# Two-layer decoder trunk: both parts of the activations in one 512-column product outside the first layer, the first tile's sums in other PSUM banks, small weights of layer 2 loaded in pieces

## The chip, the cores and the metric

One Trainium2 chip; the kernel runs on one of its cores, in one launch. The metric is the device time in microseconds (us) of the whole kernel. The engines are named as the profile names them: PE (TensorE, with PEld for its weight loads), DVE (VectorE), ACT (ScalarE), POOL (GpSimd) and SP, whose queue issues nearly all DMAs.

## What is computed

256 tokens, model width 2048, everything in float32. The first layer mixes an RWKV-7 scan (16 heads of 64) and sliding-window attention; the second is a gated unit with a 128 x 128 causal product for each of 16 channel groups. Cut to what matters here:

```
h = rmsnorm(x, e_norm)                       # layer 1
z = h @ e_w_in                               # 2048 -> 6784 columns
y = concat(rwkv7(z) * silu(..), attention(z) * silu(..))
x = x + y @ e_w_out                          # 2048 -> 2048

h = rmsnorm(x, o_norm)                       # layer 2
u, v, gate = split(h @ o_w_in, 3)            # 2048 -> 3 x 2048
v = layernorm(v, sgu_ln_w, sgu_ln_b)
mixed[g] = tril(ws[g]) @ v[:, g] + bs[g]     # 16 groups of 128 channels
x = x + (u * mixed * silu(gate)) @ o_w_out
return rmsnorm(x, final_norm)
```

## The kernel before

**Products in two parts.** Each float32 operand is split into a rounded high part and the rest: a weight chunk `raw` of 128 x 1024 (512 KB, one DMA on SP's queue) becomes `wh` (ACT, a copy) and `wl` (DVE, `raw - wh`), an activation tile of 128 x 256 becomes a high and a low tile (`xh`/`xl`, `xnh`/`xnl` after the scaling of layer 1, `x1h`/`x1l` in layer 2, `yk` and `yo` for the inputs of the two output projections). A product is then the sum of three PE matmuls: `wh` by high, `wh` by low, `wl` by high. `raw`, `wh` and `wl` have three buffers each.

**Two kinds of tiles.** A "B" tile gives 128 output columns: the weights stand in the array and the 256 tokens stream through it (function `half_b`), in two chunks of 8 steps over the contracted 2048, so 48 matmuls of 256 columns for a tile. An "A" tile gives 512 output columns for both halves of the tokens (`eighth_a`): the activations stand in the array and 512 weight columns stream, 12 matmuls of 512 columns a chunk, 8 chunks, into two accumulators `psa` and `psb`. Accumulators come from the pool `acc` (3 PSUM banks of 512 float32 columns); everything else that PE writes comes from `mis` (5 banks).

**Order.** `products` walks a list of tiles: for layer 1 an A tile (keys and values), a B tile for the two small projections, 24 B tiles for the scan, 8 B, 2 A and 8 B; then `w_out` in two passes of 16 half tiles; then layer 2's `o_in`, 4 A tiles (v) and 32 B tiles (u and gate of each group in turn); then `o_out`, 16 B tiles. After each tile a function (`e_done`, `first_done`, `resid_done`, `o_done`, `last_done`) takes the sums out of PSUM. Between the chunks `pace` lets other work (`Later`) run: generators in queues, which stop at a `Hold`. A framework then orders each engine's instructions; engines are in order.

**The start.** The first A tile's sums wait in `psa` and `psb` until the row norm `rs1`/`rc1` is known; then `kv_done` copies them out on ACT (`kd`, `v`). The next tile holds the third bank. `rms_rows` computes the norm with a scratch tile `msum` in the buffer "y", which POOL's table of angles (`rope_tables`, tiles `rt`) also uses. The small products of `lora_task` (`pw`, `pa` from `hi` and `lo`) follow the norm.

**Layer 2's small weights**: `wst` (masked by POOL), `bsb`, and four rows tiles each of `lnw` and `lnb`, are loaded after `w_out` on SP's queue, between the chunks of `o_in`. `lnw`, `lnb` are needed when the 4 A tiles are done, `wst` and `bsb` by the first gate after that.

Nearly all instructions go through a counting helper, so the profile shows line 126 for them; groups are told apart by the names of their tiles.

Of the kernel before, what the change touches and what calls it, by code (L numbers as in the profile page):

```python
# [193 lines left out]
def kernel(ctx, tc, xT, w_in, w_out, o_in, o_out, cols, rows, loras, sinks, pos, ws_t, ws_b, out, dbg=None):  # L194
# [33 lines left out]
    def k1(s, tag, dt=F32):  # L228
        return t1.tile([P, 260], dt, tag=tag, bufs=2 if tag in ("kp", "rp", "vp") else 1, name=nm(s))
# [45 lines left out]
    def half_b(pss, drams, ah, al, half, first, last):  # L275
        for ps, d in zip(pss, drams):
            wh, wl = chunk(d)
            for k in range(8):
                kt = half * 8 + k
                c = slice(k * P, (k + 1) * P)  # L280
                for i, (w, a) in enumerate(((wh, ah), (wh, al), (wl, ah))):
                    TE.matmul(ps[:, 0:T], w[:, c], a(kt), start=(first and k == 0 and i == 0),
                              stop=(last and k == 7 and i == 2))

    def first_chunk(dram):
# [8 lines left out]
        for i in range(2):  # L294
            c = slice(512 * i, 512 * i + 512)
            xh_of(i)
# [4 lines left out]
    def eighth_a(ps, dram, ah, al, q):  # L301
        wh, wl = first_chunk(dram) if not seen else chunk(dram)
        for k in range(2):
            kt = 2 * q + k
            c = slice(k * 512, (k + 1) * 512)
            for h in range(2):
                t = slice(h * P, (h + 1) * P)
                for i, (w, a) in enumerate(((wh, ah), (wh, al), (wl, ah))):
                    TE.matmul(ps[h], a(kt)[:, t], w[:, c], start=(kt == 0 and i == 0),
                              stop=(kt == NK - 1 and i == 2))  # L310

    def products(order, dram, ah, al, done, lead=0, halves=(0, 1)):
# [7 lines left out]
        def tiles(ids):  # L320
            pss = [acc("ps") for _ in ids]
            for n, half in enumerate(halves):
                end = n == len(halves) - 1
                half_b(pss, [dram[base[i] + half] for i in ids], ah, al, half, n == 0, end)
# [38 lines left out]
    xh, xl = pairs_of(NK, "xh", F32R), pairs_of(NK, "xl", F32R)  # L363
# [5 lines left out]
    def xh_of(k):  # L369
        if state.get("normed"):  # L370
            return xn[k][0]
        if k not in seen:
# [3 lines left out]
            split(xh[k], xl[k], xs[:, k], col(C_GE, k))  # L376
        return xh[k]

    def xl_of(k):
        return xn[k][1] if state.get("normed") else xl[k]  # L380
# [4 lines left out]
    def scale_task():  # L385

        for q in range(8):
# [86 lines left out]
    def setup_task():  # L474
# [13 lines left out]
        blk = const.tile([P, P], F32, name="blk")  # L488
# [4 lines left out]
        G.tensor_copy(blkr, blk)  # L493
        cen = const.tile([P, P], F32, name="cen")
# [91 lines left out]
    def ch4(ap):  # L586
        return ap.rearrange("p (c l) -> p c l", c=NCH)

# [720 lines left out]
```

## Time and profile before

| what | value |
|---|---|
| median of 3 runs | 901.04 us (898.83 to 901.15) |
| the profiled execution's own time | 904.99 us |
| its span, first to last instruction | 903.2 us |
| PE busy, with PE instructions | 870.4 us (96%), 7086 |
| DVE busy | 637.8 us (71%) |
| ACT busy | 496.8 us (55%) |
| POOL busy | 123.6 us (14%) |
| mean granted PE clock | 0.98 of full speed |

Busy time of PE counts each matmul from its start to its modelled end, and neighbours overlap, so the rate is read from how many start in a stretch. The profiled execution takes 1.8 us more than its span and 4 us more than the median of the runs.

### The profile page before, as it was taken

Reading aid. Unit: us, or ns where it says so; the run is one execution under the profiler, and the core shown is the slowest. Engines: PE = TensorE matmul, PEld = TensorE weight load, DVE = VectorE, ACT = ScalarE, POOL = GpSimd, SP = SyncE. Lnnn points to the kernel's source line nnn. Section 1 sums busy time; section 2 is a strip of 40 time slices with the busy share of each in tenths; the row PEclk is TensorE's granted clock in tenths of the full one; section 3 lists DMA queues with packets and bytes.
Section 4 is the critical chain, followed back from the end, with each engine's and each line's share of the span. In section 5 each row is a group of like instructions: output and inputs, shape, how many; then the busy total and the mean of one; then the engine's idle time right before and its main releaser. Section 6 shows DMA issues by size and latency. Waiting matters only on the chain.

```text
span 903.2 us, 17601 instructions
## 1 busy us (share of the span) xinstructions
PE 870.4 (96%) x7086; PEld 818.4 (91%) x7086; DVE 637.8 (71%) x1009; ACT 496.8 (55%) x825; POOL 123.6 (14%) x212
## 2 busy tenths in 40 slices
PE   8799999999999799999999999999999999999994
PEld 7698999999998578989999978889999999999994
DVE  6699688877999856697658955559666666655553
ACT  7587666667654387987435444447434343444441
POOL 8702000000001001000007910000000000004330
PEclk9989999999999699999999999999999999999998
DMA  7535455554366221344665866655555555656642
GB/s 274 160 117 166 151 165 164 163 159 145 117 186 184 82 91 69 94 141 164 224 195 181 303 218 196 200 188 184 171 182 175 177 173 179 180 172 186 187 164 93
DMA packets 44145, 151.68 MB, mean 168 GB/s; under 512 B 5152, under 2 KB 5536, under 8 KB 43808
## 3 DMA queue, kind: packets, MB, share of 16 engines
q1 hardware_dynamic: 43344, 149.52, 51.7%
q8 instruction: 55, 0.90, 0.4%
q10 hardware_dynamic: 720, 1.05, 0.3%
q14 instruction: 26, 0.21, 0.1%
HBM read 148.45 MB, written 2.10 MB: 167 GB/s over the span
## 4 chain that ended last, share of the span: by engine, by line
PE 77%; DVE 11%; ACT 4%; POOL 4%; issue 2%; DMA 1%; SPq 0%; DVEq 0%; ACTq 0%; POOLq 0%
PE ps L126 60%; PE psa L126 5%; PE psb L126 5%; DVE wl L126 3%; DVE dd L126 1%; ACT sc L126 1%; DMA raw<-in_o_in 1%; DVE et L126 1%; PE m L126 1%; DVE tmp L126 1%; ACT wh L126 1%; PE pm L126 1%; ACT L126 1%; DVE la L126 1%; POOL rt L552 1%
## 5 line engine op out<-in xcount | busy, mean ns | idle before, releaser
L126 ACT CAST wh<-raw 128x1024 fp32r<-128x1024 f32 (+1 forms) x267 | 278.9, 1045 | 313.7 <-PE ps L126 171.7
L126 DVE TENSOR_TENSOR wl<-raw,wh 128x1024 fp32r<-128x1024 f32 (+1 forms) x267 | 329.8, 1236 | 172.1 <-ACT wh L126 170.7
L126 PE MATMUL ps<-xnh,wh 128*128 128x256 f32 x560 | 161.8, 289 | 0.0
L126 PE MATMUL ps<-xnl,wh 128*128 128x256 f32 x560 | 159.3, 285 | 1.7 <-DVE xnl L126 1.7
L126 PE MATMUL ps<-xnh,wl 128*128 128x256 f32 x560 | 159.5, 285 | 0.7 <-DVE wl L126 0.7
L126 PE MATMUL ps<-x1h,wh 128*128 128x256 f32 x512 | 146.1, 285 | 0.0
L126 PE MATMUL ps<-x1h,wl 128*128 128x256 f32 x512 | 144.9, 283 | 0.0
L126 PE MATMUL ps<-x1l,wh 128*128 128x256 f32 x512 | 144.8, 283 | 0.0
L126 PEld LDWEIGHTS ps<-xnl,wh 128*128 128x128 f32 x560 | 107.3, 192 | 2.4 <-DVE xnl L126 2.1
L126 PEld LDWEIGHTS ps<-xnh,wh 128*128 128x128 f32 x560 | 107.4, 192 | 1.9 <-issue 1.0
L126 PEld LDWEIGHTS ps<-xnh,wl 128*128 128x128 f32 x560 | 107.3, 192 | 1.6 <-DVE wl L126 1.1
L126 PEld LDWEIGHTS ps<-x1l,wh 128*128 128x128 f32 x512 | 98.2, 192 | 0.0
L126 PEld LDWEIGHTS ps<-x1h,wh 128*128 128x128 f32 x512 | 98.2, 192 | 0.0
L126 PEld LDWEIGHTS ps<-x1h,wl 128*128 128x128 f32 x512 | 98.2, 192 | 0.0
L126 PE MATMUL ps<-yk,wh 128*128 128x256 f32 x512 | 92.8, 284 | 0.0
L126 PE MATMUL ps<-yo,wh 128*128 128x256 f32 x512 | 92.3, 283 | 0.0
L126 PEld LDWEIGHTS ps<-yk,wh 128*128 128x128 f32 x512 | 79.8, 192 | 1.1 <-DVE x L126 0.8
L126 PEld LDWEIGHTS ps<-yo,wh 128*128 128x128 f32 x512 | 79.9, 192 | 0.0
L126 PE MATMUL ps<-yo,wl 128*128 128x256 f32 x256 | 72.4, 283 | 0.0
L126 PE MATMUL ps<-yk,wl 128*128 128x256 f32 x256 | 72.4, 283 | 0.0
L126 PEld LDWEIGHTS ps<-yo,wl 128*128 128x128 f32 x256 | 49.1, 192 | 0.0
L126 PEld LDWEIGHTS ps<-yk,wl 128*128 128x128 f32 x256 | 49.1, 192 | 0.0
(327 smaller groups left out, 1479.1 us busy)
## 6 DMA issues: line engine op xcount, KB each, us to landing
raw<-in_w_in SPq DMA_DIRECT2D x105, 512.0 KB, 3.7
raw<-in_o_in SPq DMA_DIRECT2D x96, 512.0 KB, 3.6
raw<-in_w_out SPq DMA_DIRECT2D x32, 512.0 KB, 3.8
raw<-in_o_out SPq DMA_DIRECT2D x32, 512.0 KB, 3.5
x<-in_xT SPq DMA_DIRECT2D x8, 256.0 KB, 3.9
xs<-in_xT SPq DMA_DIRECT2D x7, 256.0 KB, 6.5
wst<-in_ws_t SPq DMA_DIRECT2D x1, 1024.0 KB, 5.6
bsb<-in_ws_b SPq DMA_DIRECT2D x1, 1024.0 KB, 7.6
```

The costliest lines, as they stand in the source:

```text
L126: return f(*args, **kw)
L552: G.tensor_scalar(tt, m, -part, None, op0=ALU.mult)
```

## The change

In `half_b` the first two of the three matmuls become one where `wide` is true: the activation's high and low parts now lie side by side in one tile of 128 x 512 (`parts_of`), and `wh` is multiplied with all 512 columns, into both halves of a PSUM bank. `wl` by high goes into the first half, as before. The two halves are added when the sums are taken out: `first_done` and `last_done` add twice into the residual (one more DVE operation of 128 x 256 a tile), `whole` copies one half with ACT and adds the other with DVE for u and gate. Wide are the first pass of `w_out` (128 steps), u and gate (512 steps) and `o_out` (256 steps). All of `w_in`, the second pass of `w_out` and the A tiles keep their matmuls. PE has 896 matmuls less.

The first A tile's `psa` and `psb` come from `mis` instead of `acc`. The 128 x 128 block matrix `blk` is built in the buffer "Pi" and used as its rounded copy `blkr`; "Pi" is one of the buffers of POOL's table of angles, so that POOL now builds `blk`, `blkr`, `cen` and the first `lo` at the table's end.

The small weights of layer 2 are loaded by `rows_task`, in 16 pieces of 256 KB, one after another behind chunks of `o_in`; before, they were 2 loads of 1 MB and 8 of 256 KB.

```diff
@@ -272,15 +272,20 @@
             V.tensor_tensor(wl, raw, wh.bitcast(F32), op=ALU.subtract)
         return wh, wl
 
-    def half_b(pss, drams, ah, al, half, first, last):
+    def half_b(pss, drams, xp, half, first, last, wide):
+
+
         for ps, d in zip(pss, drams):
             wh, wl = chunk(d)
             for k in range(8):
-                kt = half * 8 + k
+                x = xp(half * 8 + k)
                 c = slice(k * P, (k + 1) * P)
-                for i, (w, a) in enumerate(((wh, ah), (wh, al), (wl, ah))):
-                    TE.matmul(ps[:, 0:T], w[:, c], a(kt), start=(first and k == 0 and i == 0),
-                              stop=(last and k == 7 and i == 2))
+                if wide:
+                    TE.matmul(ps.rearrange("p (s t) -> p s t", s=2), wh[:, c], x, start=(first and k == 0), stop=False)
+                else:
+                    for s in range(2):
+                        TE.matmul(ps[:, 0:T], wh[:, c], x[:, s], start=(first and k == 0 and s == 0), stop=False)
+                TE.matmul(ps[:, 0:T], wl[:, c], x[:, 0], start=False, stop=(last and k == 7))
 
     def first_chunk(dram):
 
...
@@ -333,9 +338,10 @@
             if order[i][0] == "B":
                 tiles([i])
             else:
-                ps = (acc("psa"), acc("psb"))
+
+                ps = (mis("psa"), mis("psb")) if not seen else (acc("psa"), acc("psb"))
                 for q in range(8):
-                    eighth_a(ps, dram[base[i] + q], ah, al, q)
+                    eighth_a(ps, dram[base[i] + q], xp, q)
                     if q == 7:
                         done(i, ps)
                     pace()
...
@@ -388,10 +395,9 @@
             k = slice(2 * q, 2 * q + 2)
             (G if q % 8 < X_POOL else V).tensor_tensor(xs[:, k], xs[:, k], rs1[:, None, :].to_broadcast([P, 2, T]), op=ALU.mult)
             yield
-            h, l = pairs_of(2, "xnh", F32R), pairs_of(2, "xnl", F32R)
-            for i in range(2):
-                xn[2 * q + i] = h[i], l[i]
-                split(h[i], l[i], xs[:, 2 * q + i], col(C_GE, 2 * q + i))
+            for k, x in zip((2 * q, 2 * q + 1), parts_of(2, "xn")):
+                xn[k] = x
+                split(x[:, 0], x[:, 1], xs[:, k], col(C_GE, k))
                 yield
             yield Hold(H_XN)
 
...
@@ -485,12 +491,13 @@
             V.tensor_tensor(loras_[HS[1 - a], a], loraw[sl], loras_[sl, a].bitcast(F32), op=ALU.subtract)
         sink_b = const.tile([P, 16], F32, name="sink_b")
         load_here(sink_b, sinks.to_broadcast([P, 16]))
-        blk = const.tile([P, P], F32, name="blk")
+        blk = k1("blk", "Pi")[:, 0:P]
         G.memset(blk, 0.0)
         G.memset(blk[0:64, 0:64], 1.0)
         G.memset(blk[64:128, 64:128], 1.0)
         blkr = const.tile([P, P], F32R, name="blkr")
         G.tensor_copy(blkr, blk)
+        blk = blkr.bitcast(F32)
         cen = const.tile([P, P], F32, name="cen")
         G.tensor_scalar(cen, blk, -1.0 / HD, None, op0=ALU.mult)
         G.tensor_tensor(cen, cen, ident, op=ALU.add)
...
@@ -585,6 +592,12 @@
 
     def ch4(ap):
         return ap.rearrange("p (c l) -> p c l", c=NCH)
+
+    def whole(ps, z):
+
+        S.copy(z, ps[:, T:2 * T])
+        V.tensor_tensor(z, z, ps[:, 0:T], op=ALU.add)
+        return z
 
     def scaled(ps):
 
...
@@ -1047,8 +1060,8 @@
         th = k1("th", "kp")[:, 0:T]
         z = ps[:, 0:T]
         if rs is not None:
-            V.tensor_tensor(dst, z, rs, op=ALU.mult)
-            z = dst
+            z = whole(ps, dst)
+            V.tensor_tensor(z, z, rs, op=ALU.mult)
         S.activation(th, z, AF.Tanh, scale=0.5)
         state["tanh"] = True
         if final:
...
@@ -1109,26 +1122,27 @@
 
     later.add("r", norm_task())
     later.add("a", setup_task())
-    products(E_ORDER, w_in, xh_of, xl_of, e_done)
+    products(E_ORDER, w_in, x_of, e_done, wide=False)
 
 
     x1t = [k2("x1").rearrange("p (a t) -> p a t", a=2) for _ in range(8)]
     x1 = [x1t[i // 2][:, i % 2] for i in range(NK)]
     def first_done(i, ps):
-        V.tensor_tensor(x1[i], x1[i], ps[:, 0:T], op=ALU.add)
+        for s in range(2):
+            V.tensor_tensor(x1[i], x1[i], ps[:, s * T:(s + 1) * T], op=ALU.add)
         if i % 2 and i < NK - 1:
             load_here(x1t[i // 2 + 1], xT[:, i + 1:i + 3])
 
     load_here(x1t[0], xT[:, 0:2])
     later.finish("r")
     later.finish("n")
-    products(M_ORDER, w_out, lambda k: yk[k][:, 0], lambda k: yk[k][:, 1], first_done, halves=(0,), lead=LEAD1)
+    products(M_ORDER, w_out, lambda k: yk[k], first_done, halves=(0,), lead=LEAD1)
     later.finish()
-    x1h, x1l = pairs_of(NK, "x1h", F32R), pairs_of(NK, "x1l", F32R)
+    x1p = parts_of(NK, "x1p")
 
     def resid_done(i, ps):
         V.tensor_tensor(x1[i], x1[i], ps[:, 0:T], op=ALU.add)
-        split(x1h[i], x1l[i], x1[i], col(C_GO, i))
+        split(x1p[i][:, 0], x1p[i][:, 1], x1[i], col(C_GO, i))
         if i == 0:
             G.tensor_tensor(ssa, x1[i], x1[i], op=ALU.mult)
         else:
...
@@ -1144,23 +1158,30 @@
     lnw = [k2("lnw") for _ in range(4)]
     lnb = [k2("lnb") for _ in range(4)]
     wst, bsb = b8("wst"), b8("bsb")
-    load_here(wst, ws_t)
-    load_here(bsb, ws_b.to_broadcast([P, D]))
-    for b in range(4):
-        c = slice(512 * b, 512 * b + 512)
-        load_here(lnw[b], rows[0:1, c].to_broadcast([P, 512]))
-        load_here(lnb[b], rows[1:2, c].to_broadcast([P, 512]))
     cms = k1("cms", "aPi")[:, 0:P]
     G.memset(cms, 1.0)
     G.affine_select(cms, cms, pattern=[[1, P]], base=0, channel_multiplier=-1, compare_op=ALU.is_ge, fill=0.0)
     wst3 = wst.rearrange("p (g t) -> p g t", g=16)
-    for q in range(4):
-        G.tensor_tensor(wst3[:, 4 * q:4 * q + 4], wst3[:, 4 * q:4 * q + 4],
-                        cms[:, None, :].to_broadcast([P, 4, P]), op=ALU.mult)
     bsb3 = bsb.rearrange("p (g t) -> p g t", g=16)
     vln = b16("vln").rearrange("p (h c) -> p h c", h=2)
     bst = const.tile([P, 2, 4, 6], F32, name="bst")
     yo = {}
+
+    def rows_task():
+
+        yield Hold(3)
+        for b in range(4):
+            c = slice(512 * b, 512 * b + 512)
+            load_here(lnw[b], rows[0:1, c].to_broadcast([P, 512]))
+            yield Hold(1)
+            load_here(lnb[b], rows[1:2, c].to_broadcast([P, 512]))
+            yield Hold(1)
+            q = slice(4 * b, 4 * b + 4)
+            load_here(wst3[:, q], ws_t[:, c].rearrange("p (g t) -> p g t", g=4))
+            G.tensor_tensor(wst3[:, q], wst3[:, q], cms[:, None, :].to_broadcast([P, 4, P]), op=ALU.mult)
+            yield Hold(1)
+            load_here(bsb[:, c], ws_b[:, c].to_broadcast([P, 512]))
+            yield Hold(1)
 
     def norm2_task():
         for _ in range(3):
...
@@ -1210,12 +1231,13 @@
                 S.copy(vln[:, h, 512 * i:512 * i + 512], ps[h])
                 V.bn_stats(bst[:, h, i], vln[:, h, 512 * i:512 * i + 512])
             if i == 3:
+                later.finish("n")
                 later.add("r", ln_task(), LN_AHEAD)
             return
         g, w = (i - 4) // 2, (i - 4) % 2
         if w == 0:
             u = state["u"] = k1("uz", ("z", "y")[g % 2])[:, 0:T]
-            V.tensor_tensor(u, ps[:, 0:T], rs2, op=ALU.mult)
+            V.tensor_tensor(u, whole(ps, u), rs2, op=ALU.mult)
             return
         z = k1("gz", ("Pp", "Pi")[g % 2])[:, 0:T]
         gate(ps, rs2, z, final=(g == 15))
...
@@ -1224,13 +1246,15 @@
         sgu_task(g, state["u"], z)
 
     state["slack"] = SLACK3
-    products(O_ORDER, o_in, lambda k: x1h[k], lambda k: x1l[k], o_done)
+    later.add("n", rows_task())
+    products(O_ORDER, o_in, lambda k: x1p[k], o_done)
 
 
     last = {}
 
     def last_done(i, ps):
-        V.tensor_tensor(x1[i], ps[:, 0:T], x1[i], op=ALU.add)
+        for s in range(2):
+            V.tensor_tensor(x1[i], ps[:, s * T:(s + 1) * T], x1[i], op=ALU.add)
         if i == 0:
             G.tensor_tensor(ssa, x1[i], x1[i], op=ALU.mult)
         elif i < NK - 1:
...
@@ -1242,7 +1266,7 @@
             S.activation(last["sq"], x1[i], AF.Square)
         S.activation(x1[i], x1[i], AF.Copy, scale=col(C_GF, i))
 
-    products(M_ORDER, o_out, lambda k: yo[k][:, 0], lambda k: yo[k][:, 1], last_done, lead=LEAD4)
+    products(M_ORDER, o_out, lambda k: yo[k], last_done, lead=LEAD4)
     rms_rows([ssa, last["sq"]], rs2)
     for i in range(8):
         V.tensor_tensor(x1t[i], x1t[i], rs2[:, None, :].to_broadcast([P, 2, T]), op=ALU.mult)
```

On SP's queue, where layer 2 begins, there stood before (the last load of `w_out` first; five more loads of `lnw` and `lnb` follow the last row, and then the next `raw`):

```order
L267 DMA raw_6519<-in_w_out 128x1024
L251 DMA wst_6563<-in_ws_t 128x2048
L251 DMA bsb_6564<-in_ws_b 128x2048
L267 DMA raw_6586<-in_o_in 128x1024
L267 DMA raw_6604<-in_o_in 128x1024
L267 DMA raw_6622<-in_o_in 128x1024
L251 DMA lnw_6555<-in_rows 128x512
L251 DMA lnb_6559<-in_rows 128x512
L251 DMA lnw_6556<-in_rows 128x512
```

and now, from the fourth load of `o_in` on:

```order
L267 DMA raw_6514<-in_o_in 128x1024
L267 DMA raw_6533<-in_o_in 128x1024
L251 DMA lnw_6443<-in_rows 128x512
L251 DMA lnb_6447<-in_rows 128x512
L267 DMA raw_6552<-in_o_in 128x1024
L251 DMA wst_6451<-in_ws_t 128x512
L267 DMA raw_6572<-in_o_in 128x1024
L251 DMA bsb_6452<-in_ws_b 128x512
L267 DMA raw_6591<-in_o_in 128x1024
```

The burst of small weights behind the third load of `o_in` is gone; from the sixth load on one piece stands between two chunks.

On PE, near the end of the third tile of layer 1 (`ps_579`), where the first small products `pw` and `pa` follow, there stood before:

```order
L126 MATMUL ps_579<-xh_103,wh_701 128x256
L126 MATMUL ps_579<-xl_111,wh_701 128x256
L126 MATMUL ps_579<-xh_103,wl_702 128x256
L126 MATMUL ps_579<-xh_104,wh_701 128x256
L126 MATMUL pw_610<-hi_560,loras_344 128x256
L126 MATMUL ps_579<-xl_112,wh_701 128x256
L126 MATMUL ps_579<-xh_104,wl_702 128x256
L126 MATMUL pw_610<-lo_562,loras_344 128x256
L126 MATMUL pa_611<-hi_561,loras_344 128x256
```

and now:

```order
L126 MATMUL ps_579<-xp_110,wl_702 128x256
L126 MATMUL ps_579<-xp_111,wh_701 128x256
L126 MATMUL pw_610<-hi_560,loras_344 128x256
L126 MATMUL ps_579<-xp_111,wh_701 128x256
L126 MATMUL ps_579<-xp_111,wl_702 128x256
L126 MATMUL pw_610<-lo_562,loras_344 128x256
L126 MATMUL pa_611<-hi_561,loras_344 128x256
```

The place of `pw` is the same: 45 matmuls after the tile's first. Only the names have changed (`xp` holds both parts).

On DVE, in a group of layer 2 (`uz` and `gz` take u and gate out of PSUM, `th` is ACT's tanh, `pm` the group's 128 x 128 product), from the end of a gate tile there stood before:

```order
L126 TENSOR_TENSOR gz_8332<-ps_8271,rs_131 128x256
L126 TENSOR_TENSOR wl_8413<-raw_8410,wh_8412 128x1024
L126 SCALAR_TENSOR_TENSOR gz_8332<-th_8333,gz_8332 128x256
L126 TENSOR_TENSOR uz_8269<-uz_8269,gz_8332 128x256
L126 TENSOR_TENSOR gz_8332<-pm_8337,bsb_6564 128x256
L126 TENSOR_TENSOR uz_8269<-uz_8269,gz_8332 128x256
L126 TENSOR_TENSOR wl_8443<-raw_8440,wh_8442 128x1024
```

and now:

```order
L126 TENSOR_TENSOR gz_8000<-gz_8000,ps_7955 128x256
L126 TENSOR_TENSOR gz_8000<-gz_8000,rs_131 128x256
L126 SCALAR_TENSOR_TENSOR gz_8000<-th_8001,gz_8000 128x256
L126 TENSOR_TENSOR uz_7951<-uz_7951,gz_8000 128x256
L126 TENSOR_TENSOR gz_8000<-pm_8007,bsb_6452 128x256
L126 TENSOR_TENSOR wl_8091<-raw_8088,wh_8090 128x1024
L126 TENSOR_TENSOR uz_7951<-uz_7951,gz_8000 128x256
L126 TENSOR_TENSOR wl_8130<-raw_8127,wh_8129 128x1024
```

The first `wl` after a gate tile's end now stands behind four more operations of the gate, one of which waits for ACT's tanh; on ACT the copy out of PSUM (`COPY gz`) stands before that tanh, and the next `wh` behind it.

## Rows read from the trace of the kernel before

**Rows 1.** The page: busy us, share of the span, instructions of each engine.

```profile
PE 870.4 (96%) x7086; PEld 818.4 (91%) x7086; DVE 637.8 (71%) x1009; ACT 496.8 (55%) x825; POOL 123.6 (14%) x212
```

**Rows 2.** Stretches: us, busy of five engines (count), clock, DMA share, GB/s.

```profile
300.00:350.00 50.00, 45.89 (x593) 35.60 (x592) 31.48 (x53) 34.86 (x79) 1.50 (x4) 0.89 0.27 86
...
560.00:600.00 40.00, 40.00 (x178) 33.12 (x177) 20.49 (x19) 17.78 (x19) 0.00 (x0) 1.00 0.61 192
610.00:790.00 180.00, 180.00 (x1508) 180.00 (x1507) 124.16 (x187) 79.82 (x102) 0.00 (x0) 1.00 0.56 177
```

**Rows 3.** The chain that ended last, layer 2: start us, us, what.

```profile
565.05 0.68 PE psb L126 x3
...
785.93 11.51 PE ps L126 x96
797.89 92.17 PE ps L126 x768
```

**Rows 4.** Waits of PE: us in total, times, longest.

```profile
PE psa L126 <- ACT wh L126: 4.0, 4, 1.7
...
PE ps L126 <- ACT v L126: 3.4, 1, 3.4
```

**Rows 5.** The same chain at layer 2's beginning.

```profile
514.85 0.51 SPq L251
...
515.46 9.15 DMA raw<-in_o_in
...
524.71 1.05 ACT wh L126
```

**Rows 6.** Stretches behind PE's wait of layer 2, columns as in rows 2.

```profile
505.00:510.00 5.00, 5.00 (x44) 5.00 (x43) 4.97 (x5) 1.58 (x3) 4.92 (x4) 1.00 1.00 418
...
526.00:528.00 2.00, 2.00 (x5) 1.61 (x6) 1.97 (x4) 1.97 (x4) 0.00 (x0) 0.50 0.04 14
528.00:530.00 2.00, 2.00 (x8) 1.55 (x8) 2.00 (x3) 0.46 (x1) 0.00 (x0) 0.71 0.83 193
```

**Rows 7.** PE in order of time, layer 1: start us, us, instruction, [idle before <-releaser].

```profile
45.14 0.58 PE L126 MATMUL ps<-xh,wh 128*128 128x256 f32 x1 [3.36 <-ACT v L126]
...
53.10 0.28 PE L126 MATMUL pw<-hi,loras 128*128 128x256 f32 x1
...
88.78 0.55 PE L126 MATMUL ps<-xnl,wh 128*128 128x256 f32 x1 [1.45 <-DVE xnl L126]
```

**Rows 8.** DVE in order of time, layer 1.

```profile
39.66 0.42 DVE L126 TENSOR_SCALAR msum<-rms 128x256 f32<-128x256 f32 x1 [4.26 <-POOL rt L570]
...
51.13 0.86 DVE L126 TENSOR_TENSOR lo<-zp,hi 64x256 fp32r<-64x256 f32 x2
```

**Rows 9.** Stretches of layer 1, columns as in rows 2.

```profile
46.00:48.00 2.00, 2.00 (x11) 2.00 (x11) 2.00 (x5) 1.98 (x4) 0.00 (x0) 0.50 0.62 209
...
50.00:55.00 5.00, 5.00 (x39) 5.00 (x39) 3.98 (x9) 3.75 (x9) 0.00 (x0) 0.87 0.30 108
```

**Rows 10.** POOL in order of time, at the beginning.

```profile
8.46 0.45 POOL L496 TENSOR_TENSOR cen<-cen,ident 128x128 f32<-128x128 f32 x1
...
14.62 0.60 POOL L610 CAST lo<-blk 64x256 fp32r<-64x256 f32 x1
```

**Rows 11.** DVE in order of time, the end of one gate tile.

```profile
689.84 0.42 DVE L126 TENSOR_TENSOR gz<-ps,rs 128x256 f32<-128x256 f32 x1 [0.65 <-PE ps L126]
690.80 1.23 DVE L126 TENSOR_TENSOR wl<-raw,wh 128x1024 fp32r<-128x1024 f32 x1 [0.54 <-ACT wh L126]
```

**Rows 12.** Groups of DVE by shape: busy us, mean ns | idle before.

```profile
L126 DVE TENSOR_TENSOR gz<-pm,bsb 128x256 f32<-128x256 f32 x16 | 6.8, 425 | 1.6
```

**Rows 13.** Groups of ACT by shape, columns as in rows 12.

```profile
L126 ACT CAST wh<-raw 128x1024 fp32r<-128x1024 f32 x265 | 277.6, 1048 | 312.3 <-PE ps L126 171.7 <-issue 69.6 <-PE psb L126 41.9
...
L126 ACT ACTIVATE th<-gz 128x256 f32<-128x256 f32 x16 | 6.6, 415 | 0.0
```

**Rows 14.** ACT in order of time: a copy of 128 x 256 out of PSUM.

```profile
44.62 0.47 ACT L126 ACTIVATE v<-psa,rc 128x256 f32<-128x256 f32 x1
```

More of the change, by code (lines that the diff above doesn't have):

```diff
@@ L228, in k1 @@
     def k1(s, tag, dt=F32):
-        return t1.tile([P, 260], dt, tag=tag, bufs=2 if tag in ("kp", "rp", "vp") else 1, name=nm(s))
+        return t1.tile([P, 260 if tag == "Pp" else T], dt, tag=tag, bufs=2 if tag in ("kp", "rp", "vp") else 1, name=nm(s))
     def tiny(s):
@@ L295, in first_chunk @@
             c = slice(512 * i, 512 * i + 512)
-            xh_of(i)
+            x_of(i)
             S.copy(wh[:, c], raw[:, c])
@@ L299, in first_chunk, with eighth_a @@
         return wh, wl
-    def eighth_a(ps, dram, ah, al, q):
+    def eighth_a(ps, dram, xp, q):
         wh, wl = first_chunk(dram) if not seen else chunk(dram)
@@ L307, in eighth_a, with products @@
                 t = slice(h * P, (h + 1) * P)
-                for i, (w, a) in enumerate(((wh, ah), (wh, al), (wl, ah))):
-                    TE.matmul(ps[h], a(kt)[:, t], w[:, c], start=(kt == 0 and i == 0),
+                for i, (w, s) in enumerate(((wh, 0), (wh, 1), (wl, 0))):
+                    TE.matmul(ps[h], xp(kt)[:, s, t], w[:, c], start=(kt == 0 and i == 0),
                               stop=(kt == NK - 1 and i == 2))
-    def products(order, dram, ah, al, done, lead=0, halves=(0, 1)):
+    def products(order, dram, xp, done, lead=0, halves=(0, 1), wide=True):
         base, at = [], 0
@@ L323, in tiles @@
                 end = n == len(halves) - 1
-                half_b(pss, [dram[base[i] + half] for i in ids], ah, al, half, n == 0, end)
+                half_b(pss, [dram[base[i] + half] for i in ids], xp, half, n == 0, end, wide)
                 for i, ps in zip(ids, pss):
@@ L361, in col, with parts_of @@
         return colt[lo:hi, base + j:base + j + 1]
-    xh, xl = pairs_of(NK, "xh", F32R), pairs_of(NK, "xl", F32R)
+    def parts_of(n, s):
+        return [k2(s, F32R).rearrange("p (s t) -> p s t", s=2) for _ in range(n)]
+    xp = parts_of(NK, "xp")
     def split(dst_h, dst_l, src, g):
@@ L367, in split, with x_of @@
         V.scalar_tensor_tensor(dst_l, src, g, dst_h.bitcast(F32), op0=ALU.mult, op1=ALU.subtract)
-    def xh_of(k):
+    def x_of(k):
         if state.get("normed"):
-            return xn[k][0]
+            return xn[k]
         if k not in seen:
@@ L375, in xh_of @@
                 load_x(q)
[L376 to L380, printed above, removed]
+            split(xp[k][:, 0], xp[k][:, 1], xs[:, k], col(C_GE, k))
+        return xp[k]
     seen = set()
@@ L1137, in resid_done @@
             G.tensor_tensor(ssa, ssa, sq, op=ALU.add)
-    products(M_ORDER, w_out, lambda k: yk[k][:, 0], lambda k: yk[k][:, 1], resid_done, halves=(1,), lead=LEAD2)
+    products(M_ORDER, w_out, lambda k: yk[k], resid_done, halves=(1,), lead=LEAD2, wide=False)
     rs2 = rs1
```

## The prediction, made before the kernel ran

> **What bounds the kernel now.** I read the page's first part, then the stretches, then PE's waits, and only then the chain and the time lines of the two places where PE waited.
>
> PE is busy 96% of the span [rows 1], but its busy time overlaps itself, so the rate says more. Where layer 2 computes u and gate, PE starts 1508 matmuls in 180 us at full clock and is never idle; DVE is busy 124 of these 180 us, ACT 80, the DMA engines 56% [rows 2]. So PE's own work sets the time there. The chain says what one matmul costs: 768 of 256 columns in 92.17 us, or 120.0 ns each, and 3 of 512 columns in 0.68 us, or 226.7 ns each [rows 3]. The 106.7 ns between them are the price of 256 more columns; what is left over, 120.0 - 106.7 = 13.3 ns, comes once for each matmul, long or short. Before 400 us it is different in places: between 300 and 350 us PE is idle for 4 us and at 0.89 of its clock [rows 2]; there the scan's small steps set the pace, which the change doesn't touch.
>
> PE's two longest waits lie outside all this: 3.4 us for ACT's copy `v` in layer 1 and 1.7 us for a `wh` where layer 2 begins [rows 4].
>
> **Term 1: 896 matmuls less, 11.9 us less.** A step had three matmuls of 256 columns, 3 x 120.0 = 360.0 ns. Now it has one of 512 and one of 256: 226.7 + 120.0 = 346.7 ns, 13.3 ns less. With 128 + 512 + 256 = 896 such steps that is 11.9 us. The 512-column rows are of the A tiles, in which weights stream past activations; here activations stream past weights, in the same type and number of columns. No row shows just this product, so I bound it: not under 2 x 106.7 = 213.4 ns (columns alone), not over 2 x 120.0 = 240.0 ns (no better than the two it replaces). The saving lies between 0 and 23.8 us; the A tiles' row is by far the nearest, and I take it. Little of the 11.9 can be lost to other engines: 10.2 us of it fall into layer 2, where PE never waits.
>
> The Trainium skill, "TensorE: Matmul & The Clock Gate", section "Back-to-back issue gap", gives a warm gap of columns / 2.4 + 2.5 ns. The trace agrees with its price for columns and not with its fixed part: 13.3 ns stand here in place of 2.5. By that section a matmul less would be worth 2.5 ns and the 896 together 2.2 us; the rows decide for 13.3.
>
> **What pays for it.** Adding the halves costs DVE one more operation of about 0.43 us a tile [rows 12] and, for u and gate, ACT a copy out of PSUM of 0.47 us [rows 14]. For a group of two tiles that is 0.9 us more on each. DVE's 124 of 180 us [rows 2] are 8.3 us for the 12.0 us of a group (15 groups in the 180 us); 9.2 us still fit into the new 11.6 us. ACT goes from 5.3 to 6.2 us. Both stay behind PE. At the very end nothing covers it: the last tile's second addition comes after the last matmul and before the final norm, plus 0.4 us.
>
> **Term 2: the small weights in pieces, 3.3 us less.** SP issues eight loads of rows one after another ahead of the next `raw`, which it can issue only at 515.46; with 4 MB on the way it takes 9.15 us to land, and `wh` begins at 524.71 [rows 5]. The DMA engines moved 418 GB/s at the height of the burst [rows 6]. PE waits 1.7 us [rows 4] and then finds itself at half clock: 0.50 for 2 us and 0.71 for 2 us [rows 6], which gives away 1.0 + 0.6 us. With pieces of 256 KB between chunks of 512 KB the queue has to bring 768 KB in the 2.72 us of a chunk (12 x 226.7 ns), or 289 GB/s, below the 418 shown. A piece ahead of a chunk holds it up by 0.9 us at this rate; the three buffers of split chunks leave PE two more chunks, 5.4 us, to go on with, so that is hidden. The last piece stands behind the 19th of 32 chunks, so POOL's masking, now behind its last sum of squares, has over 30 us until the first gate. The sixteen loads are six issues more on SP, of about 0.5 us each [rows 5]. If a piece came late after all, the price is up to these same 3.3 us.
>
> **Term 3: other banks for the first tile, 1.0 us less.** This is where I expect little. PE waited 3.36 us for a bank, until ACT had copied `v` at 45.1 [rows 7], and ran at half clock until about 51.3 (0.50, then 0.87 over 5 us) [rows 9], which cost 3.1 us more: 6.5 us in all. Now the third bank is free and PE goes on at 41.8. But 45 matmuls on stands `pw`, at the same place of PE's order. It waits for `lo`, which DVE ended at 52.0 [rows 8] and PE used at 53.10 [rows 7]. `lo` comes from the norm, and the norm's `msum` waits for POOL's table, not for PE [rows 8]. PE reaches `pw` at 41.8 + 45 x 0.120 = 47.2 and waits there instead. What shortens this chain is POOL alone: `cen`'s second step and the first `lo` (0.45 + 0.60 us, [rows 10]) now come after the table, so `msum` and `lo` come about 1 us earlier, `lo` at 51.0. The new wait is then 3.8 us long, and as the clock fell in the 3.4 us wait it should fall here. What is late next is `lo` on DVE, then the normalised activations: PE waits again at 88.78 for `xnl` [rows 7], and these now stand before `z` in DVE's order. I take 1.0 us for all of it; the ends are 0 and the full 6.5.
>
> **Sum.** -11.9 - 3.3 - 1.0 + 0.4 = -15.8 us. The profiled execution took 904.99 us, 1.8 more than its span and 4.0 more than the median; from 904.99 it would come to 889.2, and from the median of 901.04 to **885.2 us**.
>
> **Rivals.**
>
> *The long product costs what its two halves did* (the change does not do what it says). Then term 1 is nothing: -3.3 - 1.0 + 0.4 = -3.9, 897.1 us. For it: nothing streams activations of 512 columns in the trace. Against it: the A tiles show 512 columns at 226.7 with a change of the standing operand before each [rows 3], as here. Chance 0.10. By the gap of the Trainium skill's page, 2.2 us of term 1 would be left, and the time 894.9 us; the 13.3 ns of the rows are against that too.
>
> *The first layer gives back everything.* If PE's matmuls before `pw` keep the clock up, or DVE works faster without PE behind it, term 3 is -6.5 in place of -1.0: 879.7 us. Against it: `lo` hangs on `msum`, and that on POOL [rows 8]. Chance 0.13.
>
> *Slower: the gate's chain holds back `wl`.* In each group the first `wl` behind a gate tile now stands behind the sum's chain. Before it began 1.0 us after the tile's end [rows 11]. Now: ACT's copy 0.47, two DVE operations 0.85, tanh 0.42 [rows 13], three DVE operations 1.28, so it begins at 3.0 and ends at 4.2 us (a `wl` is 1.23 long, [rows 11]). Its chunk is the third from there, needed two chunks, 16 x 0.3467 = 5.5 us, and 0.2 us of the pair of products `pm` after the tile's end: cover 1.5 us. If the copy stands behind a `wh` (1.05 us, [rows 13]), the first addition behind a `wl` (1.23) and the tanh behind another `wh` (1.05), the chain is 3.3 us longer, PE waits 1.8 us in each of 16 groups, 28.8 us: 914.0 us. It makes the kernel slower from 15.8 / 16 = 1.0 us of waiting a group, a chain 2.5 us longer than summed. Against it: in the listing no `wh` stands between copy and tanh, and DVE has time. Chance 0.05.
>
> **How the numbers follow.** My forecast has a chance of 0.70, the three rivals 0.10, 0.13 and 0.05, and 0.02 is left for others. The forecast's own range is 882 to 890 (1 us either way for the A tiles' row, up to 3.3 us for a late piece, 2 us for term 3). For 8 in 10 it is widened to the second rival's 879.7 and a little over the forecast's upper end: 879 to 892; the first and the third stay outside. No change to be told is within 0.3%, 2.7 us, of 901.04. Faster: forecast, second rival, most of the first, 0.90. Slower: 0.05. The same: 0.05.
>
> **What would show it.** Right: in the chain of layer 2 a tile of u takes 32 matmuls and 5.55 us instead of 5.76, PE without a wait and at full clock from 450 us to the end; no wait of `psa` for `wh` where layer 2 begins; in layer 1 no wait for `v`, but one of 3 to 4 us for `lo` or `hi` before `pw`, and a half clock behind it. Wrong: a 512-column product over 235 ns; a wait of PE for `wl` in each group; a `raw` of `o_in` that lands later than 8 us; or PE at 63 us more than 2 us ahead of before.

## The result, and the profile after

The changed kernel takes **887.09 us** (886.77 to 888.06), the kernel before 900.32 in the same runs: a ratio of 0.9857 [0.9839, 0.9874], 13.2 us or 1.5% less. I had forecast 885.2, with a range of 879 to 892. The profiled execution took 888.06 us, with a span of 886.3.

First the stretches of [rows 2] in the changed kernel, with the whole of 450 to 850 us below; columns are length, busy time and count of PE, its weight load, DVE, ACT and POOL, granted clock, DMA share and GB/s.

```profile
560.00:600.00 40.00, 40.00 (x181) 33.18 (x180) 20.23 (x20) 17.91 (x21) 0.00 (x0) 1.00 0.59 192
610.00:790.00 180.00, 180.00 (x1056) 158.29 (x1055) 133.78 (x214) 85.83 (x127) 0.00 (x0) 1.00 0.59 182
...
450.00:850.00 400.00, 400.00 (x2323) 352.64 (x2322) 279.59 (x392) 191.23 (x256) 66.79 (x56) 1.00 0.62 196
```

PE is never idle and at full clock for the whole 400 us; DVE and ACT have taken on more and stay behind it. The weight load, which filled all 180 us before, now has 22 us to spare.

The chain that ended last, where layer 2 begins, in its groups of u and gate, and in `o_out` (start, us, what, number of instructions):

```profile
382.00 5.75 PE ps L126 x48
...
510.17 0.69 PE psa L126 x3
...
598.16 11.29 PE ps L126 x64
...
621.54 11.30 PE ps L126 x64
...
633.29 11.10 PE ps L126 x64
...
644.83 11.10 PE ps L126 x64
...
656.38 11.30 PE ps L126 x64
...
784.16 88.77 PE ps L126 x512
874.34 0.71 PE rms L126 x2
```

A group of two tiles has 64 products where [rows 3] had 96, and ten of the 16 groups take 11.10 us: 5.55 a tile, as forecast. Six take 11.30, every third from the third on, and the first. `o_out` went from 92.17 to 88.77 us, 3.4 less. Between the last product and `rms` there are now 874.34 - 784.16 - 88.77 = 1.41 us.

PE's waits (us in total, times, longest), then PE in order of time, layer 1:

```profile
PE psa L126 <- ACT wh L126: 3.1, 3, 2.1
PE pw L126 <- ACT hi L126: 3.0, 1, 3.0
...
PE ps L126 <- DVE xn L126: 1.2, 2, 0.9
```

```profile
49.57 0.38 PE L126 MATMUL pw<-hi,loras 128*128 128x256 f32 x1 [3.05 <-ACT hi L126]
```

The wait for `v` of [rows 4, 7] is gone, and 3.05 us stand before `pw` in its place. The `psa` row is the very first tile, from 5 to 12 us; from 450 to 850 us PE waits for nothing. Behind `pw` the clock falls to half, 1.2 GHz, as the stretches show:

```profile
48.00:50.00 2.00, 0.43 (x3) 0.41 (x3) 1.97 (x5) 1.88 (x6) 0.00 (x0) 1.00 0.28 55
50.00:52.00 2.00, 2.00 (x11) 1.93 (x10) 1.97 (x5) 2.00 (x4) 0.00 (x0) 0.52 0.55 215
52.00:54.00 2.00, 2.00 (x13) 2.00 (x13) 2.00 (x4) 1.58 (x5) 0.00 (x0) 0.62 0.00 0
```

### The profile page after: what moved, and what is told of

Its sections match the earlier page's. It is cut to its first block, busy times and chain, and to the rows that moved or that the text cites. A ratio compares the mean times of both kernels' runs of the same rounds, so it can differ in the third digit from the quotient of the medians.

```text
span 886.3 us, 15898 instructions
## 1 busy us (share of the span) xinstructions
PE 857.0 (97%) x6190; PEld 765.9 (86%) x6190; DVE 659.1 (74%) x1073; ACT 504.2 (57%) x857; POOL 127.3 (14%) x212
## 4 chain that ended last, share of the span: by engine, by line
PE 79%; DVE 10%; ACT 5%; POOL 4%; issue 2%; DMA 0%; DVEq 0%; POOLq 0%; ACTq 0%
PE ps L126 60%; PE psa L126 6%; PE psb L126 5%; DVE wl L126 3%; DVE dd L126 1%; ACT sc L126 1%; DVE et L126 1%; PE m L126 1%; ACT L126 1%; DVE tmp L126 1%; PE pm L126 1%; ACT wh L126 1%; PE ptp L126 1%; POOL rt L567 1%; PE psc L126 1%
## 5 line engine op out<-in xcount | busy, mean ns | idle before, releaser
L126 PE MATMUL ps<-xn,wh 128*128 128x256 f32 x1120 | 207.2, 286 | 1.2 <-DVE xn L126 1.2
L126 PE MATMUL ps<-x1p,wh 128*128 128x512 f32 x512 | 180.8, 397 | 0.0
L126 PEld LDWEIGHTS ps<-xn,wh 128*128 128x128 f32 x1120 | 174.8, 192 | 4.1 <-DVE xn L126 2.0
L126 PE MATMUL ps<-xn,wl 128*128 128x256 f32 x560 | 158.9, 284 | 0.7 <-DVE wl L126 0.7
L126 PE MATMUL ps<-x1p,wl 128*128 128x256 f32 x512 | 143.2, 280 | 0.0
L126 PEld LDWEIGHTS ps<-x1p,wh 128*128 128x128 f32 x512 | 96.1, 188 | 21.8
L126 PEld LDWEIGHTS ps<-xn,wl 128*128 128x128 f32 x560 | 107.2, 192 | 1.6 <-DVE wl L126 1.1
L126 PEld LDWEIGHTS ps<-x1p,wl 128*128 128x128 f32 x512 | 96.6, 189 | 0.0
L126 PE MATMUL ps<-yk,wh 128*128 128x256 f32 (+1 forms) x384 | 92.0, 323 | 0.0
L126 PE MATMUL ps<-yo,wh 128*128 128x512 f32 x256 | 88.9, 391 | 0.0
```

What stands on the lines that cost most here:

```text
L126: return f(*args, **kw)
```

## The experiments

All times are medians (range) of runs beside the kernel before on the same chip. The kernel before had medians of 900.65, 901.83 and 900.61 in the three sets.

| kernel | us | ratio to the kernel before |
|---|---|---|
| before_again | 899.87 | 0.9998 |
| after_again | 887.75 (887.33 to 889.36) | 0.9865 [0.9848, 0.9881] |
| undo_wide | 897.44 (895.9 to 898.22) | 0.9967 [0.9956, 0.9978] |
| undo_pieces | 894.41 (893.81 to 895.2) | 0.9934 [0.992, 0.9949] |
| pieces_only | 898.01 (896.62 to 900.06) | 0.9959 [0.9945, 0.9973] |
| undo_banks | 887.62 (886.66 to 891.05) | 0.9853 [0.983, 0.9876] |
| undo_blk | 889.41 (887.39 to 891.73) | 0.9883 [0.9864, 0.9902] |
| undo_early | 889.37 (887.92 to 890.88) | 0.9878 [0.9859, 0.9896] |
| lora_later | 887.24 (886.73 to 887.98) | 0.9841 [0.982, 0.9862] |
| quarter | 943.99 (943.88 to 944.09) | 1.0471 [1.0434, 1.0508] |
| resid_wide | 886.79 (886.68 to 887.17) | 0.9851 [0.9833, 0.987] |
| all_wide | 895.2 (894.7 to 896.79) | 0.9946 [0.9931, 0.9962] |

### Both kernels again

No edit.

> The kernel before once more, for a second profile of it. The first profiled execution took 904.99 us where its runs have a median of 900.3, and its first 90 us hold a bank wait of 3.4 us and stretches at half clock. If those 4 us belong to that one execution, this profile has a span near 899 us and reaches the first tile with normalised activations (88.78 us there) up to 4 us earlier, by a shorter half clock. If they belong to the kernel under the profiler, the span is 903 again and the place is at 88 to 89 us.

> The changed kernel once more, on the same chip as the two that undo a part of it. Expected 886 to 888 us and a ratio of 0.985 to before.

Both medians held. The new profile of the kernel before took 899.61 us and not 904.99, and its chain reaches the first run of 48 products behind the norm at 97.53 us, where the first profile had 100.49 and the changed kernel has 96.58 and 96.32. So a part of what two profiles show as a gain in layer 1 is the difference between two executions. The profile of the changed kernel shows another such difference, in the groups and in `o_out`:

```profile
644.44 11.30 PE ps L126 x64
...
783.78 90.46 PE ps L126 x512
```

Here the whole of `o_out` took 90.46 us where the first profile had 88.77, at a clock of 1.00 until 850 us in both. A step of one 512-column and one 256-column product takes 88.77 / 256 = 346.8 ns in one and 90.46 / 256 = 353.4 ns in the other. The groups show the same two rates: 11.10 / 32 = 346.9 and 11.30 / 32 = 353.1 ns.

### The long products undone

```diff
                 if wide:
-                    TE.matmul(ps.rearrange("p (s t) -> p s t", s=2), wh[:, c], x, start=(first and k == 0), stop=False)
+                    for s in range(2):
+                        TE.matmul(ps[:, s * T:(s + 1) * T], wh[:, c], x[:, s],
+                                  start=(first and k == 0 and s == 0), stop=False)
```

> The changed kernel with two 256-column products in place of each 512-column one, into the same two halves of the bank; the additions, copies, banks and loads stay. If a product costs 13.3 ns beside its columns, 896 more of them are 11.9 us: 899 us, of which 10.2 us in layer 2, a tile of u or gate at 5.76 us on PE again in place of 5.55. If the fixed part is the 2.5 ns of the Trainium skill's gap, 2.2 us: 889 us. If the saving is lost to other engines in part, less than 11.9.

897.44 us: 9.7 more than the changed kernel beside it. The chain, set against the first profile of the changed kernel, gives the same sum by stage:

```profile
382.45 5.75 PE ps L126 x48
...
511.44 0.69 PE psa L126 x3
...
599.43 11.51 PE ps L126 x96
...
790.94 92.17 PE ps L126 x768
884.52 0.71 PE rms L126 x2
```

From 382 us to layer 2's first `psa` it takes 128.99 us against 128.17, 0.8 more; the 16 groups 191.51 against 186.00, 5.5 more; `o_out` 3.4 more: 9.7 in all. Between the last product and `rms` it has the same 1.41 us as the changed kernel, since the additions are still there.

Term 1 had 13.3 ns for each of 128 + 512 + 256 steps. `o_out` gave 13.3 in the first profile. Six of the 16 groups ran at 353 ns and gave 6.7: 16 x 32 x 13.3 ns less 6 x 32 x 6.6 ns is 5.5 us. The first pass of `w_out` gave 0.82 us / 128 = 6.4 ns. That is the whole difference to 11.9. The sum by stage hangs on the execution, though: in the second profile of the changed kernel `o_out` ran at the slower rate throughout and gave 1.7 us in place of 3.4, which makes 8.0 us. At either rate the long product is the cheaper one; the exact agreement with the medians is partly luck.

### Pieces: undone, and alone

```diff
     wst, bsb = b8("wst"), b8("bsb")
+    load_here(wst, ws_t)
+    load_here(bsb, ws_b.to_broadcast([P, D]))
+    for b in range(4):
+        c = slice(512 * b, 512 * b + 512)
+        load_here(lnw[b], rows[0:1, c].to_broadcast([P, 512]))
+        load_here(lnb[b], rows[1:2, c].to_broadcast([P, 512]))
```

with the loads taken out of `rows_task` (undo_pieces). The other kernel, pieces_only, is the kernel before with `rows_task` in place of those lines, and nothing else of the change.

> The changed kernel with the small weights of layer 2 loaded in the burst of before. If the burst costs what the trace of before shows, 1.7 us of waiting and 1.6 us of half clock, it takes 3.3 us more, 890.5 us, with PE waiting for wh where layer 2 begins and the clock at 0.5 behind it. If the wait there was of one execution only, or PE would have run into another wait anyway, 0 to 1 us more.

> The kernel before with one part of the change alone: the small weights of layer 2 come in pieces, spread over its first products. My term 2 expects 3.3 us less than the kernel before (1.7 of waiting at the first psa of layer 2 and 1.6 of half clock behind it), so about 897.2, with no wait of PE for wh between 500 and 545. The rival takes the figure that undoing this part in the changed kernel gave (6.7 us): about 893.8. If it is near 3, the larger figure belongs to the place that the burst gets in the changed kernel, where SP issues it behind five chunks of o_in and not behind three.

Undone, the pieces cost 6.7 us, twice the forecast; alone on the kernel before they gave 3.7 (2.4 to 5.0 by the interval). SP's queue tells why. First the kernel before (before_again), then undo_pieces (start, us, line, what, number):

```profile
499.09 6.50 SPq L267 DMA_DIRECT2D raw<-in_o_in  x3
505.64 0.42 SPq L251 DMA_DIRECT2D lnw<-in_rows  x1
...
511.34 27.16 SPq L267 DMA_DIRECT2D raw<-in_o_in  x11
```

```profile
498.32 14.61 SPq L267 DMA_DIRECT2D raw<-in_o_in  x5
512.99 0.43 SPq L251 DMA_DIRECT2D lnw<-in_rows  x1
...
518.32 21.51 SPq L267 DMA_DIRECT2D raw<-in_o_in  x8
```

In undo_pieces the eight loads of rows stand behind five chunks of `o_in`, not three. They start 7 us later, and so does the chunk behind them, which PE needs. That chunk takes 9.02 us to land (9.09 in before_again), and PE waits 4.73 us, where before_again waits 1.71, and runs at half clock after that:

```profile
528.54 1.22 PE L126 MATMUL psa<-wh,x1p 128*128 128x512 f32 x2 [4.73 <-ACT wh L126]
```

```profile
528.00:530.00 2.00, 1.43 (x3) 0.71 (x4) 1.45 (x2) 1.58 (x3) 0.00 (x0) 0.63 0.10 39
530.00:532.00 2.00, 2.00 (x5) 1.61 (x6) 1.96 (x2) 1.00 (x1) 0.00 (x0) 0.51 0.63 119
```

By their clock the two stretches lose at most 0.37 and 0.49 of 2 us each, 1.7 us, which with the wait makes 6.4. So the 6.7 us are the price of another burst than the one of before. What the pieces save there is seen in the chain, from a column tile of `w_out` to the first whole group of layer 2 that it shows, in before_again, in pieces_only and in the first profile of before:

```profile
432.43 5.75 PE ps L126 x48
...
601.15 11.51 PE ps L126 x96
```

```profile
435.36 5.75 PE ps L126 x48
...
601.87 11.51 PE ps L126 x96
```

```profile
436.60 5.75 PE ps L126 x48
...
606.53 11.51 PE ps L126 x96
```

168.72 us became 166.51, 2.2 less; the first profile of before has 169.93 there, 3.4 more than pieces_only. Both profiles of before have the same wait (1.74 and 1.71 us). The 1.2 us between them go with the half clock behind the wait, which [rows 6] show and before_again does not (1.00 from 510 to 530 us).

### The first layer: banks and POOL's order

```diff
-                ps = (mis("psa"), mis("psb")) if not seen else (acc("psa"), acc("psb"))
+                ps = (acc("psa"), acc("psb"))
```

is undo_banks;

```diff
-        blk = k1("blk", "Pi")[:, 0:P]
+        blk = const.tile([P, P], F32, name="blk")
...
-        blk = blkr.bitcast(F32)
```

is undo_blk, which gives POOL the order of before; undo_early has both. In lora_later, the changed kernel with `H_LO = 2` in place of 1, the products of `pw` and `pa` stand later in PE's order, but only by five products, not by the twenty of the expectation.

> The changed kernel with the two halves of the first tile back in the three banks that the column tiles use. My term 3 expects 1.0 us more than the changed kernel (range 0 to 6.5), with PE waiting at the next column tile for the copy of v, as before, and no longer for 3 us at pw. The rival: the wait at pw only takes the place of the wait for v, the copy of lo sets both, and the time is the same within 0.3 us.

> The changed kernel with the block of ones in a tile of its own again, so that POOL comes to its parts in the order of before. In the changed kernel POOL's last cast of lo began at 42.69, in the kernel before at 43.94, 1.25 later. If this and not the banks is what the first layer gained, it costs about 1.0 to 1.3 us against the changed kernel (888.1 to 888.5 where that takes 887.2), with the cast of lo at about 43.9. The rival (the order on POOL is hidden by the wait at pw): same within 0.3 us.

> Both changes to the first layer undone: the block of ones in a tile of its own and the first tile in the banks of the column tiles. Term 3 as predicted (all of the first layer's gain is 1.0) expects 1.0 more than the changed kernel. If the parts measured so far (long products 9.7, pieces 3.7 on the kernel before) make up all of the 12.9 to 13.4 us, nothing is left for the first layer: same within 0.5 us.

> The changed kernel with the products of pw and pa some twenty products later in PE's order. If the 3.05 us wait at pw and the half clock behind it are now what the first layer loses, PE fills the time with column products: 3 to 5 us less than the changed kernel at the first ps of the third tile (96.6 us) and about as much at the end. The rival: the gates that hang on pw come later by as much, and PE waits for them further on (v, lo or xn): same within 0.5 us or slower.

Other banks are worth nothing that can be told: 887.62 without them against 887.09 and 887.75, and 889.37 against 889.41 with POOL's old order. In PE's order of time, first undo_banks, then undo_blk, which has the new banks:

```profile
43.06 0.51 PE L126 MATMUL ps<-xp,wh 128*128 128x256 f32 x2 [1.21 <-ACT v L126]
49.09 0.39 PE L126 MATMUL pw<-hi,loras 128*128 128x256 f32 x1 [0.61 <-ACT hi L126]
```

```profile
50.00 0.39 PE L126 MATMUL pw<-hi,loras 128*128 128x256 f32 x1 [3.04 <-ACT hi L126]
```

In undo_banks PE waits twice, 1.21 us for `v` and 0.61 for `pw`, and keeps the full clock from 40 to 60 us; in the changed kernel it waits once, 3.05 us, and drops to half. That is one execution: undo_early, with the same old banks, waits 3.67 us for `v` and runs at half clock behind it, as before did. `pw` is reached at 49.09 in undo_banks and 49.57 in the changed kernel: the row names ACT's `hi`, which comes from the norm, and nothing done to PE's order moves that. lora_later says the same: PE does more before `pw`, waits 2.38 us in place of 3.05 and goes on at 49.21. It reaches the place that the changed kernel has at 96.58 and 96.32 at 95.75, not 3 to 5 us earlier, and the time stays.

POOL's order is what moved the norm. Its `msum` waits for POOL's table (DVE in order of time) in the changed kernel, in undo_blk and in undo_early:

```profile
38.07 0.42 DVE L126 TENSOR_SCALAR msum<-rms 128x256 f32<-128x256 f32 x1 [3.37 <-POOL rt L577]
```

```profile
38.51 0.42 DVE L126 TENSOR_SCALAR msum<-rms 128x256 f32<-128x256 f32 x1 [3.10 <-POOL rt L576]
```

```profile
39.48 0.42 DVE L126 TENSOR_SCALAR msum<-rms 128x256 f32<-128x256 f32 x1 [4.59 <-POOL rt L576]
```

The kernels with POOL's new order have `msum` at 37.6 to 38.1 us, those with the old one at 38.5 to 39.7. In all eleven profiles in which PE waits at `pw`, `pw` begins 11.5 us behind `msum`, whatever the banks. (POOL's last cast of `lo`, of which the expectations speak, waits for the norm's `rc`, so it only marks the same shift: 42.2 to 42.7 us against 43.1 to 44.3.) By medians the old order costs 1.7 to 2.3 us (889.4 against 887.1 to 887.8), and by the ratios 1.2 to 2.3, which counts for more here: undo_blk and undo_early ran on another chip than after_again. The intervals of the ratios overlap, so I take the sign as likely and the size as rough.

### How short may a product be

```diff
+                if wide == 4:
+                    xf = x.rearrange("p s t -> p (s t)")
+                    for s in range(4):
+                        TE.matmul(ps[:, s * P:(s + 1) * P], wh[:, c], xf[:, s * P:(s + 1) * P],
+                                  start=(first and k == 0 and s == 0), stop=False)
...
-    products(M_ORDER, o_out, lambda k: yo[k], last_done, lead=LEAD4)
+    products(M_ORDER, o_out, lambda k: yo[k], last_done, lead=LEAD4, wide=4)
```

> The changed kernel with each 512-column product of o_out as four products of 128 columns, 256 steps in all, weights and sums the same. If a product costs its columns and 13.3 ns, as term 1 has it, a step goes from 346.7 ns to 4 x 66.7 + 120.0 = 386.7, 10.2 us more in all. If a gap of 2.5 ns is all that a product pays, 1.9 us more. If a product can't be shorter than its weight load lets it be, the nearest row is that of the four 128-column products of pm, 0.44 us or 110 ns each: a step of 560 ns, 54.6 us more.

943.99 us, 56.2 to 56.9 more than the changed kernel: the third answer. A stretch of `o_out` in this kernel:

```profile
800.00:900.00 100.00, 100.00 (x889) 100.00 (x887) 37.34 (x47) 29.18 (x34) 27.39 (x23) 1.00 0.37 117
```

889 products in 100 us are 112.5 ns each, four of five with 128 columns, and the weight load is busy for all 100 us. "Its columns and 13.3 ns" would make 66.7 ns of 128 columns. Most likely the load that goes with each product doesn't let it. That is read from the row and not tested by itself; a least time of 112 ns for any product is ruled out by the solve, where products of 32 columns with 32 x 32 weights start every 37 ns (94 in 3.52 us, in all_wide's row below). The Trainium skill, "TensorE: Matmul & The Clock Gate", section "LDWEIGHTS (loading the stationary operand)", gives a load the time columns / 1.2, an estimate of 107 ns for 128; the spacing comes near that, with 112.5. A single load shows 191 ns in this trace, but neighbours overlap, so only the spacing can be set beside it.

### Long products elsewhere

resid_wide uses them in the second pass of `w_out`:

```diff
-        V.tensor_tensor(x1[i], x1[i], ps[:, 0:T], op=ALU.add)
+        for s in range(2):
+            V.tensor_tensor(x1[i], x1[i], ps[:, s * T:(s + 1) * T], op=ALU.add)
...
-    products(M_ORDER, w_out, lambda k: yk[k], resid_done, halves=(1,), lead=LEAD2, wide=False)
+    products(M_ORDER, w_out, lambda k: yk[k], resid_done, halves=(1,), lead=LEAD2)
```

all_wide adds the tiles of layer 1 from the eighth on (`wide` is then the number of the first wide tile; the other lines of the edit only pass it on):

```diff
-            z = shift(ps if i >= X_NEW else scaled(ps), ...)
+            z = shift(whole(ps, k1("z", "z")[:, 0:T]) if i >= X_NEW else scaled(ps), ...)
...
-        z = ps[:, 0:T]
+        z = whole(ps, dst)
         if rs is not None:
-            z = whole(ps, dst)
...
-    products(E_ORDER, w_in, x_of, e_done, wide=False)
+    products(E_ORDER, w_in, x_of, e_done, wide=X_NEW)
```

> The changed kernel with 512-column products in the second pass of w_out too: 128 products fewer and one more addition on DVE for each of its 16 tiles. PE is busy throughout that stretch (70.00 of 70 us between 440 and 510), so 13.3 ns for each product give 1.7 us less than the changed kernel (about 885.5). The rival: the addition stands in the path from the last tile to the first product of layer 2, and 0.4 us of it or more comes back.

> As the one before, and 512-column products also in the 35 column tiles of the first layer from the eighth on, with one copy on ACT and one addition on DVE more for each tile: 560 products fewer. Where PE is the bound throughout, 13.3 ns for each give 7.5 us, with the second pass 9.2 us: about 878. PE has all 80 us from 90 to 170 but only 123 of 130 from 170 to 300, so I expect 4 to 7 us in all (880 to 883). The rival: the gates and the scan hang on DVE and ACT there, the extra 0.9 us for each tile comes on their chains, and only the 1.7 us of the second pass is left, or less.

resid_wide took 886.79 us, 0.3 to 1.0 less than the changed kernel, where I had expected 1.7. Its products in `w_out`, from the chain:

```profile
438.43 70.87 PE ps L126 x400
```

400 products are 200 steps, 354 ns each: the slower rate again, so a step saves about half of 13.3 ns, or 0.9 us in 128 steps. Its first `psa` of layer 2 comes 510.17 - 509.30 = 0.9 us earlier. It is the fastest of all kernels here, by less than can be told.

all_wide is 8 us slower than the changed kernel. One head of layer 1 takes longer, 20.11 us for 19.78 (first all_wide, then resid_wide):

```profile
115.99 5.65 PE ps L126 x32
...
136.10 5.66 PE ps L126 x32
```

```profile
115.71 5.76 PE ps L126 x48
...
135.49 5.75 PE ps L126 x48
```

16 steps went from 5.75 to 5.65 us, again 353 ns a step, and the small products between them took more than that back. At 261 us the two kernels are level (261.25 and 261.33). Then the solve's first products wait for DVE, behind the scores `sc` of the attention:

```profile
302.58 3.52 PE L126 MATMUL px<-et,Tm 32*32 32x32 f32 x94 [7.96 <-DVE sc L126]
```

```profile
300.00:305.00 5.00, 2.42 (x77) 2.42 (x78) 4.94 (x8) 0.56 (x1) 0.00 (x0) 0.50 0.01 3
```

In resid_wide the same products wait for DVE too, but less, and begin 11 us earlier:

```profile
291.54 2.50 PE L126 MATMUL px<-et,Tm 32*32 32x32 f32 x126 [1.91 <-DVE et L126]
```

resid_wide has other waits and half clock behind it there, so the whole 11 us are not lost: at the solve's second half all_wide is 5.2 us behind (313.10 against 307.93), and at 455 us 8.1. The first 5.2 us go with that wait and the half clock behind it; where the other 3 arise, in the scan and attention after it, was not followed. So my rival held for all_wide, with its place in the solve and behind it.

## Why the prediction was right, point by point

**Term 1** (11.9 us) was right in kind and 2.2 us too large. A step costs what the A tiles' row makes of it, 346.7 ns, only at the faster of two rates; `w_out` and six of 16 groups ran at the slower one, where a step saves about 6.7 ns. Measured: 0.8 + 5.5 + 3.4 = 9.7 us, by the stages and by the medians (8.0 by the stages of the execution with the slower `o_out`). I had no row for the product and took the nearest one as it stood. "A 512-column product over 235 ns" was a sign of being wrong. The step less 120.0 ns makes 227 and 233; by the starts themselves the long product takes 230 ns at the faster rate and 236 at the slower one, the short one 117. So the sign showed, by 1 ns, where the slower rate held. The forecast was 887.09 - 885.2 = 1.9 us too low, but it was counted from a median of 901.04, and the kernel before then had 900.32: of the gain, 15.8 us were forecast and 13.2 came.

**The first rival** (the long product saves nothing) fell, and the 2.5 ns of the Trainium skill's section with it: 2.2 us for 896 products, where 9.7 were measured. (The section itself calls that gap the one of an isolated product; here a weight load goes with each.) But the fixed 13.3 ns, which I had used against it, is only the price at 256 and 512 columns: at 128 the spacing is 112.5 ns, most likely set by the weight load.

**What pays for it** held. DVE has 133.78 of 180 us and ACT 85.83, and PE waits for neither. At the end the gap before `rms` went from 891.01 - 797.89 - 92.17 = 0.95 us ([rows 3], and the same chain's `rms` below) to 1.41, the 0.4 forecast.

```profile
891.01 0.71 PE rms L126 x2
```

**Term 2** (3.3 us) held: 2.2 to 3.4 us at its place, 3.7 by the medians of pieces_only. PE doesn't wait at layer 2's beginning and no piece came late.

**Term 3** (1.0 us) held in its mechanism, with the wrong part named in its title. The wait moved from `v` to `pw`, 3.05 us where I had 3.8: I had let `pw` wait for `lo`, but the row at 53.10 in [rows 7] is already `pw` from `hi`, which is ready sooner. The clock fell behind the wait in both profiles of the changed kernel, but not in undo_blk behind the same wait, so that part of the forecast had luck in it. It cost little at its place: undo_wide, whose clock stayed full there, is at the place of 96.58 and 96.32 at 96.53. The banks gave nothing that can be told; the order on POOL, which I had counted with them, most likely gave the term, at 1.2 to 2.3 us rather than 1.0. One sign of being wrong showed here: the 314th product on PE, which the changed kernel starts at 63.07 us, had started at 65.31 in the first profile of before, 2.2 us later where I had allowed 2. Against before_again (63.94) it is 0.9 us, so most of the 2.2 belongs to that one execution. **The second rival** (6.5 us) did not come about, for the reason given: the norm hangs on POOL.

**The slower rival** (the gate's chain holds back `wl`) did not come about: no wait of PE for `wl` in 400 us.

The parts add up to 9.7 + 2.2 to 3.7 + 1.2 to 2.3 - 0.4 = 12.7 to 15.3 us, against 12.9 to 13.2 for the whole. So term 1 came out smaller than forecast and term 3 probably larger, and part of the nearness of the sum is that they offset each other. The upper end is more than was there; I did not settle whether that is the medians' uncertainty, which is some 1.5 us in each difference, or two parts that save the same time.

## What to carry to other kernels

Where PE is the bound and never idle, count products, not only columns: one of 512 columns was 6.7 to 13.3 ns cheaper than two of 256, and one of 128 cost nearly as much as one of 256. The same edit where small products and other engines' chains stand between the long ones lost 8 us, so it goes stage by stage. When a part is undone in the changed kernel, look first where its instructions now stand in the queues: the burst put back was twice as dear as the burst that had been there.

## What was not expected of the hardware

A step of a 512-column and a 256-column product ran at 346.8 or at 353.2 ns, at a granted clock of 1.00 in both. A whole stretch keeps one rate and the next may have the other: `o_out` had 346.8 in one execution of the same program and 353.4 in another, 1.7 us apart, and six groups of 16 had the slower one in the first profile. The groups take turns: in all ten profiles with long products in the groups, from the third group on just one in three is slow. In nine of them it is the third, sixth and so on, and `o_out`, the stretch behind the 16th group, is fast where it has these steps; in after_again the turn came one group earlier, so that `o_out` fell on the slow one. Three 256-column products never showed this (11.51 us in every group of undo_wide). What sets the rate, and why by threes, stays open.

A single wait of 3.05 us was followed by half clock (0.52 and 0.62 in the next two stretches), while two waits of 1.21 and 0.61 us in the same place were not. Nor was the single wait of 3.04 us in undo_blk (1.00 from 40 to 60 us), so the length of the wait alone does not say whether the clock falls. By the medians both cost the same in the end.
